# Conversions of low-rank weights and rotations of queries and keys, issued at later places and in program order

## The chip, the cores and the metric

One Trainium2 chip, one of its cores. The time is device microseconds (us) of one execution of the whole program, for an input of 256 tokens; lower is better. The engines: TensorE (PE in the profile; PEld is its weight load), VectorE (DVE), ScalarE (ACT), GpSimd (POOL) and SyncE (SP, whose queue issues all DMAs here).

## The reference

A trunk of two layers, 2048 wide. Each layer normalises, projects once, runs two groups of heads beside each other, gates both, projects back and adds:

```
for l in range(2):
    h = rms_norm(x, norm_g[l]);  proj = h @ w_in[l]
    rw_in, g_rw, q, k_at, v_at, g_at = split(proj)
    r, k, v, xw, xa = split(bidir_token_shift(rw_in, shift_mu[l]))
    # A) RWKV-7 mixing, one scan per direction d, 16 heads of 64
    decay = exp(-exp(-softplus(-(w0[d] + tanh(xw) @ decay_up[d])) - 0.5))   # decay_up: 96 x 1024
    a     = sigmoid(a0[d] + xa @ iclr_up[d])                                # iclr_up:  96 x 1024
    S = S*decay - (S@kk) (a*kk)^T + v k^T ;  y = S@r        # delta rule, forward and reversed, summed
    # B) windowed attention, 16 query heads, 4 key heads, sink logit
    qh, kh = rope(q), rope(k_at)        # [t1*cos - t2*sin, t2*cos + t1*sin] on halves of 32
    y_at = softmax_with_sink(qh kh^T / 8, |i-j| <= 128) @ v_at
    x = x + concat(y_rw * silu(g_rw), y_at * silu(g_at)) @ w_out[l]
out = rms_norm(x, final_g)
```

## The kernel before

Everything is kept transposed: 128 channels on the partitions, 256 tokens along the free axis. Every float32 product is made of three fp32r matmuls on a high and a low part of each operand: `hi` is a rounded copy made by ScalarE, `lo` = value − `hi`, made by VectorE.

**The stream of projections.** `gemm` is one output tile of 128 channels: 16 steps of three matmuls (L286 to L288) into one of two PSUM buffers `pm`. Its weights come in two halves of 512 KB (`raw<-wi`, three buffers), which `wsplit` turns into `hi` (L216, two calls of 128x512) and `lo` (L218), two buffers of each. `S.run(n)` issues the next n steps; `S.later(n, fn)` calls `fn` after the n-th step from there, the running one counted. When a tile's last step is issued its `evac` is called: it reads `pm` and frees it.

**The scans.** `window(64, ...)` issues 64 steps of the stream in 14 groups and between them the pieces of the scans: `scan_p` (decay, rates and keys of one pair of heads), `scan_i` (inverse of the triangular systems) and `scan_b` (state). Window w projects k, v, r and the gate of pair p = w; in it `scan_p` of pair w − 1 runs, so the low-rank product `pza` of pair w − 1 (L636 to L638) is some 16 steps into window w. `pza` is followed on ScalarE by `lw`, `th`, `t` and `kkr`, and on VectorE by a long chain from `lw<-lw` to the product behind `pbn`; PE needs `t` for `pk` (L642, first use) and the end of VectorE's chain for `pbn` (L642, second use). After the eight pairs come the tiles of k (two) and q (eight) of the attention, whose evacuation rotates them.

**What sets the order.** PE runs in program order. The other queues are ordered by a list scheduler, which places an instruction as soon as its model of the machine has the inputs ready and the engine free, the earlier in the program first. `PA` and `PV` are ScalarE and VectorE with one rule more: an instruction issued through them stays behind the instruction that the program issued before it on that engine. In the profile, all that goes through them has line L231. `scan_p` and part of the others use `PA` and `PV`.

**The two places of the change.** `ups` (L472) fetches the low-rank weights of a pair, `g<-iup` (96 rows) and `g<-dup` (97 rows), at the start of its k tile; `value_evac`, at the end of its v tile, evacuates v and converts both into `iuh`, `iu`, `duh`, `du` with `split` (L455 on ScalarE, L456 on VectorE). The buffers `g` are two, shared with the gates (`g`, `th` in `silu_evac`) and with the angles of `setup`, which make `SIN` and `COS` in window 0. `rope_evac` copies `pm` to `u` (L506), has four DMAs swap its halves into `rrot` (L508), turns on VectorE (L509 to L511) and converts (L513 on ScalarE, L514 on VectorE). All of these use the plain `A` and `V`.

Of the kernel before, what the change touches and what calls it, by code (L numbers as in the profile page):

```python
# [9 lines left out]
F32 = mybir.dt.float32  # L10
# [5 lines left out]
AF = mybir.ActivationFunctionType  # L16
ALU = mybir.AluOpType
# [112 lines left out]
def hybrid_trunk_kernel(ctx, tc, xT, wi, wv, wo, par, fing, dup, iup, sink, pos, cst, out):  # L130
    nc = tc.nc
    V, A, G, PE, SY = nc.vector, nc.scalar, nc.gpsimd, nc.tensor, nc.sync
# [22 lines left out]
    def st(tag, shape, dt=F32, bufs=1):  # L155
        return sp.tile([128, *shape], dt, tag=tag, name=tag, bufs=bufs)
# [76 lines left out]
    PA, PV = InTurn(A), InTurn(V)  # L233
# [36 lines left out]
    S = Stream()  # L270
# [130 lines left out]
    def queue_inputs(l):  # L401
# [7 lines left out]
        def shift_evac(j, place):  # L409
            def evac(pm):  # L410
                dst = place()
                u = st("u", [T], bufs=2)
                V.tensor_tensor(u, pm, L.norm.rb, op=ALU.mult)
                A.activation(dst, u, AF.Identity, scale=dpm(0, j))
                V.scalar_tensor_tensor(dst[:, 1:T], u[:, 0 : T - 1], prm(P_MU0, j), dst[:, 1:T], op0=ALU.mult, op1=ALU.add)
                V.scalar_tensor_tensor(dst[:, 0 : T - 1], u[:, 1:T], prm(P_MU1, j), dst[:, 0 : T - 1], op0=ALU.mult, op1=ALU.add)

            return evac
# [11 lines left out]
        def new(t, name, tag, bufs):  # L430
            def place():
                t[name] = st(tag, [T], bufs=bufs)
                return t[name]

            return place
# [17 lines left out]
        def split(hl, x, rows):  # L453
            hi, lo = (a[0:rows] for a in hl)
            A.activation(hi, x[0:rows], AF.Copy)  # L455
            V.tensor_tensor(lo, x[0:rows], hi.bitcast(F32), op=ALU.subtract)  # L456
# [19 lines left out]
        def value_evac(p, t):  # L476
            ev = shift_evac(8 + p, new(t, "v", "vg", 8))

            def evac(pm):
                ev(pm)  # L480
                for n, rows in (("iu", RANK), ("du", RANK + 1)):
                    raw = t[n]
                    t[n] = (st(n + "h", [2, 128], F32R), st(n, [2, 128], F32R))
                    split(t[n], raw, rows)

            return evac

# [9 lines left out]
        def rope_evac(place):  # L497
            def evac(pm):
                if not rope:
                    rope.extend((st("TW", [T]), st("XA", [T])))  # L500
                    V.tensor_tensor(rope[0], COS, L.norm.rb, op=ALU.mult)
                    V.tensor_tensor(rope[1], SIN, L.norm.rb, op=ALU.mult)
                CR, SR = rope
                raw = st("u", [T], bufs=2)
                rot = st("rrot", [T])
                A.activation(raw, pm, AF.Copy)  # L506
                for q in range(4):
                    SY.dma_start(out=rot[q * 32 : q * 32 + 32, :], in_=raw[(q ^ 1) * 32 : (q ^ 1) * 32 + 32, :])  # L508
                V.tensor_tensor(raw, raw, CR, op=ALU.mult)  # L509
                V.tensor_tensor(rot, rot, SR, op=ALU.mult)  # L510
                V.tensor_tensor(raw, raw, rot, op=ALU.add)  # L511
                hi, lo = place()
                A.activation(hi, raw, AF.Copy)  # L513
                V.tensor_tensor(lo, raw, hi.bitcast(F32), op=ALU.subtract)  # L514

            return evac

# [650 lines left out]
```

## Time and profile before

| | us |
|---|---|
| median of 3 runs | 1235.19 (1234.38 to 1235.47) |
| the profiled execution: its time | 1234.27 |
| its span | 1232.4 |
| PE busy | 1182.2 |
| DVE busy | 930.7 |
| ACT busy | 743.0 |
| DMA queue of SP, share of the 16 engines' span | 41.0% |

The span is the time from the first to the last instruction; 1.9 us lie around it. Rows of the timeline begin with start and duration in us; in brackets at the end is how long the engine had stood idle before and what ended that. In the rows by stretches, PEclk is the granted clock of TensorE as a share of full speed. A row of the waits gives the total in us, the number of times, and the longest.

### The profile page before, as it was taken

Reading aid. Unit: us, or ns where it says so; the run is one execution under the profiler, and the core shown is the slowest. Engines: PE = TensorE matmul, PEld = TensorE weight load, DVE = VectorE, ACT = ScalarE, POOL = GpSimd, SP = SyncE. Lnnn points to the kernel's source line nnn. Section 1 sums busy time; section 2 is a strip of 40 time slices with the busy share of each in tenths; the row PEclk is TensorE's granted clock in tenths of the full one; section 3 lists DMA queues with packets and bytes.
Section 4 is the critical chain, followed back from the end, with each engine's and each line's share of the span. In section 5 each row is a group of like instructions: output and inputs, shape, how many; then the busy total and the mean of one; then the engine's idle time right before and its main releaser. Section 6 shows DMA issues by size and latency. Waiting matters only on the chain. (4 is left out here: it accounts for less than half of the span.)

```text
span 1232.4 us, 38183 instructions
## 1 busy us (share of the span) xinstructions
PE 1182.2 (96%) x16204; PEld 1096.3 (89%) x16204; DVE 930.7 (76%) x2067; ACT 743.0 (60%) x1838; POOL 19.1 (2%) x23
## 2 busy tenths in 40 slices
PE   6989999999999899999998999999999999999996
PEld 6978998999998889999998889999999888899996
DVE  7878778887876668856676788878887866786654
ACT  6546665766665567655555556675776565665553
POOL 0000000000000000000000000000000000000000
PEclk9999999999999999999999999999999999999998
DMA  7433333323323334467654333333323333445653
GB/s 249 157 136 116 105 117 109 105 96 114 119 89 99 117 112 144 140 214 240 209 182 147 124 128 93 106 111 111 105 94 106 124 102 127 131 130 178 211 192 121
DMA packets 60411, 166.72 MB, mean 135 GB/s; under 512 B 7728, under 2 KB 22736, under 8 KB 60240
## 3 DMA queue, kind: packets, MB, share of 16 engines
q1 hardware_dynamic: 60240, 164.27, 41.0%
q8 instruction: 127, 2.08, 0.7%
q14 instruction: 44, 0.36, 0.1%
HBM read 157.43 MB, written 4.19 MB: 131 GB/s over the span
## 5 line engine op out<-in xcount | busy, mean ns | idle before, releaser
L286 PE MATMUL pm<-XH,hi 128*128 128x256 f32 x1664 | 498.8, 300 | 9.4 <-ACT XH L179 5.9
L288 PE MATMUL pm<-XH,lo 128*128 128x256 f32 x1664 | 471.5, 283 | 4.8 <-DVE lo L218 4.6
L287 PE MATMUL pm<-XL,hi 128*128 128x256 f32 x1664 | 471.8, 284 | 0.1
L216 ACT ACTIVATE hi<-raw 128x512 fp32r<-128x512 f32 x560 | 328.1, 625 | 238.0 <-PE pm L287 147.9
L218 DVE TENSOR_TENSOR lo<-raw,hi 128x512 fp32r<-128x512 f32 x560 | 368.4, 687 | 96.7 <-ACT hi L216 89.2
L286 PEld LDWEIGHTS pm<-XH,hi 128*128 128x128 f32 x1664 | 317.3, 191 | 34.9 <-issue 13.0
L288 PEld LDWEIGHTS pm<-XH,lo 128*128 128x128 f32 x1664 | 318.3, 191 | 6.5 <-DVE lo L218 6.4
L287 PEld LDWEIGHTS pm<-XL,hi 128*128 128x128 f32 x1664 | 318.3, 191 | 0.9 <-DVE XL L180 0.9
L286 PE MATMUL pm<-MH,hi 128*128 128x256 f32 x512 | 144.1, 281 | 1.2 <-ACT hi L216 1.2
L288 PE MATMUL pm<-MH,lo 128*128 128x256 f32 x512 | 143.9, 281 | 0.4 <-DVE lo L218 0.4
L287 PE MATMUL pm<-ML,hi 128*128 128x256 f32 x512 | 143.8, 281 | 0.0
L286 PEld LDWEIGHTS pm<-MH,hi 128*128 128x128 f32 x512 | 96.6, 189 | 2.2 <-ACT hi L216 1.4
L288 PEld LDWEIGHTS pm<-MH,lo 128*128 128x128 f32 x512 | 96.6, 189 | 0.6 <-DVE lo L218 0.6
L287 PEld LDWEIGHTS pm<-ML,hi 128*128 128x128 f32 x512 | 96.6, 189 | 0.0
L908 ACT ACTIVATE suv<-pcc 64x128 f32<-64x128 f32 x128 | 34.2, 267 | 18.1 <-PE pq L835 11.8
L837 ACT ACTIVATE QF<-pq 128x256 f16<-128x256 f32 x80 | 30.8, 385 | 19.8 <-PE pq L835 19.0
L993 ACT ACTIVATE mv<-mv,mx 128x257 f32<-128x257 f32 x64 | 32.0, 503 | 17.5 <-DVE mx L990 17.3
L740 DVE TENSOR_TENSOR ge<-pg,C 128x1024 f32<-128x1024 f32 x32 | 39.1, 1221 | 3.2 <-PE pg L734 3.1
L844 DVE CAST_PREDICATED tv<-LV,pd 128x256 f16<-128x256 uint8 x80 | 34.4, 430 | 7.7 <-PE pd L843 6.9
L892 ACT ACTIVATE rh<-pcc 128x128 f32<-128x128 f32 x64 | 17.5, 273 | 35.4 <-PE pcc L890 35.0
L734 PE MATMUL pg<-mv,bk 64*128 64x128 f32 x512 | 37.2, 285 | 0.0
L845 DVE CAST_PREDICATED tt<-LV,pd 128x256 f16<-128x256 uint8 x80 | 34.1, 426 | 0.0
(239 smaller groups left out, 1845.8 us busy)
## 6 DMA issues: line engine op xcount, KB each, us to landing
raw<-wi SPq DMA_DIRECT2D x207, 512.0 KB, 3.3
raw<-wo SPq DMA_DIRECT2D x64, 512.0 KB, 4.3
raw<-wv SPq DMA_DIRECT2D x8, 512.0 KB, 3.3
rrot<-u SPq DMA_DIRECT2D x80, 32.0 KB, 2.0
vg<-xT SPq DMA_DIRECT2D x16, 128.0 KB, 4.6
xd<-vg SPq DMA_DIRECT2D x16, 128.0 KB, 2.4
vg<-xd SPq DMA_DIRECT2D x16, 128.0 KB, 3.3
g<-dup SPq DMA_DIRECT2D x16, 97.0 KB
```

The lines of the kernel that those rows point to most:

```text
L216: A.activation(hi[:, q], raw[:, q], AF.Copy)
L218: V.tensor_tensor(lo[:, q], raw[:, q], hi[:, q].bitcast(F32), op=ALU.subtract)
L286: PE.matmul(pm, wh, rh[:, kk, :], start=(kk == 0), stop=False)
L287: PE.matmul(pm, wh, rl[:, kk, :], start=False, stop=False)
L288: PE.matmul(pm, wl, rh[:, kk, :], start=False, stop=(kk == 15))
L734: PE.matmul(pg[:, h, c * 128 : (c + 1) * 128], BK[half[h], d, c, 1 - h : 3 - h, :].rearrange("p s j -> p (s j)"), MV[half[h], d, c].rearra ...
L740: V.tensor_tensor(GEd(d), pg.rearrange("p h (c x) -> p h c x", c=NC), gm[d].unsqueeze(1).unsqueeze(1).to_broadcast([128, 2, NC, 128]), op= ...
L837: A.activation(t_sub(QF), flat4(pq[:, :, 0:128]), AF.Copy)
L844: V.copy_predicated(t_sub(TC), t_mask, flat4(pd[:, :, 0:128]))
L845: V.copy_predicated(v_sub(TT), v_mask, flat4(pd[:, 0, 128:384].rearrange("p (d x) -> p d x", d=2)))
L908: A.activation(here(h), pc[half[h], 1], AF.Copy)
L993: A.activation(Sc[:, h, q, 0:257], Sc[:, h, q, 0:257], AF.Exp, scale=0.125, bias=mx[:, q : q + 1], accum_out=den[:, q : q + 1])
```

## The change

The conversions of the low-rank weights are issued five steps after the evacuation of v instead of with it, and through `PA` and `PV`. The rotation is issued six steps after the copy to `u` and its conversion nine steps after, through `PA` and `PV` as well; the copy and the four DMAs stay. No instruction of a computation is added or removed.

```
         def value_evac(p, t):
             ev = shift_evac(8 + p, new(t, "v", "vg", 8))
-            def evac(pm):
-                ev(pm)
+            def parts():
                 for n, rows in (("iu", RANK), ("du", RANK + 1)):
                     raw = t[n]
                     t[n] = (st(n + "h", [2, 128], F32R), st(n, [2, 128], F32R))
-                    split(t[n], raw, rows)
+                    hi, lo = (a[0:rows] for a in t[n])
+                    PA.activation(hi, raw[0:rows], AF.Copy)
+                    PV.tensor_tensor(lo, raw[0:rows], hi.bitcast(F32), op=ALU.subtract)
+            def evac(pm):
+                ev(pm)
+                S.later(6, parts)
...
         def rope_evac(place):
                 A.activation(raw, pm, AF.Copy)
                 for q in range(4):
                     SY.dma_start(out=rot[q * 32 : q * 32 + 32, :], in_=raw[(q ^ 1) * 32 : (q ^ 1) * 32 + 32, :])
-                V.tensor_tensor(raw, raw, CR, op=ALU.mult)
-                V.tensor_tensor(rot, rot, SR, op=ALU.mult)
-                V.tensor_tensor(raw, raw, rot, op=ALU.add)
                 hi, lo = place()
-                A.activation(hi, raw, AF.Copy)
-                V.tensor_tensor(lo, raw, hi.bitcast(F32), op=ALU.subtract)
+                def turn():
+                    PV.tensor_tensor(raw, raw, CR, op=ALU.mult)
+                    PV.tensor_tensor(rot, rot, SR, op=ALU.mult)
+                    PV.tensor_tensor(raw, raw, rot, op=ALU.add)
+                def parts():
+                    PA.activation(hi, raw, AF.Copy)
+                    PV.tensor_tensor(lo, raw, hi.bitcast(F32), op=ALU.subtract)
+                S.later(7, turn)
+                S.later(10, parts)
```

PE's order stays. The order on ScalarE changes at the start of the first layer, where `rb` is the scale of the norm, which every evacuation there waits for. The rows of ScalarE before, with the conversions of pair 0:

```order
L1065 ACTIVATE mv<-X_87 128x1024
L216 ACTIVATE hi<-raw 128x512 x4
L455 ACTIVATE iuh<-g 96x256
L455 ACTIVATE duh<-g 97x256
L204 ACTIVATE rb<-pb 128x256
L216 ACTIVATE hi<-raw 128x512
```

And now:

```order
L1077 ACTIVATE mv<-X_87 128x1024
L216 ACTIVATE hi<-raw 128x512 x4
L204 ACTIVATE rb<-pb 128x256
L216 ACTIVATE hi<-raw 128x512
L414 ACTIVATE kr<-u,DP 128x256 x2
```

`rb` is no longer queued behind the two conversions; those now stand behind the evacuation of v of pair 0, `vg<-u`. In the second layer the pair that stood between the weight halves of the output projection went to the same place.

On ScalarE at the change from the first window to the second, in the first layer, the rows before were these (`duh` and `iuh` are pair 1's, `pza` is pair 0's):

```order
L358 ACTIVATE COS<-COS 128x256
L425 ACT_TABLE_LOAD
L425 ACTIVATE g<-g 128x256
L216 ACTIVATE hi<-raw 128x512 x4
L414 ACTIVATE kr<-u,DP 128x256
L455 ACTIVATE duh<-g 97x256
L455 ACTIVATE iuh<-g 96x256
L231 ACTIVATE lw<-pza 128x512
```

And now:

```order
L425 ACT_TABLE_LOAD
L425 ACTIVATE g<-g 128x256
L216 ACTIVATE hi<-raw 128x512 x2
L358 ACT_TABLE_LOAD
L358 ACTIVATE COS<-COS 128x256
L414 ACTIVATE kr<-u,DP 128x256
L231 ACT_TABLE_LOAD
L231 ACTIVATE lw<-pza 128x512
```

The two conversions have gone to a place behind `lw<-th`, fourteen rows further, and `COS` has come between the gate and `lw<-pza`, with two table loads more: the angles wait for the buffers `g`, which pair 0's conversions now free later. On VectorE `iu` and `du` of pair 1 have moved from ahead of `lw<-lw` into its chain, between `bk<-th` and `lw<-lw,kr`. The second layer has the same move without `COS` and the loads.

On VectorE at the first rotation of k (in each layer), before:

```order
L231 SCALAR_TENSOR_TENSOR lw<-lw,PR,kr 128x256
L509 TENSOR_TENSOR u<-u,TW 128x256
L510 TENSOR_TENSOR rrot<-rrot,XA 128x256
L932 TENSOR_SCALAR yv<-yv 128x4
L511 TENSOR_TENSOR u<-u,rrot 128x256
L231 TENSOR_TENSOR ysq<-py,yv 128x256
L218 TENSOR_TENSOR lo<-raw,hi 128x512
L514 TENSOR_TENSOR kd<-u,KA 128x256
L218 TENSOR_TENSOR lo<-raw,hi 128x512
L844 COPY_PREDICATED tv<-LV,pd 128x2x4x32
```

And now:

```order
L231 SCALAR_TENSOR_TENSOR lw<-lw,PR,kr 128x256
L231 TENSOR_TENSOR u<-u,TW 128x256
L231 TENSOR_TENSOR rrot<-rrot,XA 128x256
L944 TENSOR_SCALAR yv<-yv 128x4
L231 TENSOR_TENSOR u<-u,rrot 128x256
L218 TENSOR_TENSOR lo<-raw,hi 128x512 x2
L231 TENSOR_TENSOR kd<-u,KA 128x256
L231 TENSOR_TENSOR ysq<-py,yv 128x256
L856 COPY_PREDICATED tv<-LV,pd 128x2x4x32
```

The turn `u<-u,TW` stands where it stood; `ysq`, which waits for GpSimd's `yv`, has gone behind both weight halves and the conversion. On SP one weight load (`raw<-wi`) has moved ahead of the first fetch of pair 1 in the first layer, and in each layer one ahead of the four DMAs of the fourth rotation.

## The prediction

> **What bounds the kernel now.** I read the page's first part, then the waits of PE, then the timeline around the longest of them.
>
> ```profile
> span 1232.4 us, 38183 instructions
> PE 1182.2 (96%) x16204; PEld 1096.3 (89%) x16204; DVE 930.7 (76%) x2067; ACT 743.0 (60%) x1838; POOL 19.1 (2%) x23
> ```
>
> PE is busy for all but 50.2 us of the span, and its order and work don't change. So only its pauses, and a clock below full speed, can give time back.
>
> ```profile
> PE pbn L642 <- DVE lw L231: 5.6, 2, 2.8
> PE pk L642 <- ACT t L231: 5.4, 2, 2.9
> PE pm L288 <- DVE lo L218: 4.9, 7, 1.5
> PE pf L851 <- DVE tt L845: 3.5, 2, 2.4
> PE pq L835 <- DVE tv L844: 3.5, 4, 1.0
> PE pf L851 <- DVE tv L844: 2.7, 2, 1.5
> ```
>
> These are few and long, once or twice a layer. The timeline of PE says where they are:
>
> ```profile
> 29.28 0.38 PE L286 MATMUL pm<-XH,hi 128*128 128x256 f32 x1 [1.62 <-DVE u L413]
> 69.07 0.65 PE L642 MATMUL pk<-t,C 64*64 64x256 f32 x4 [2.92 <-ACT t L231]
> 85.59 0.65 PE L642 MATMUL pbn<-lw,C 64*64 64x256 f32 x4 [2.77 <-DVE lw L231]
> 548.36 0.39 PE L286 MATMUL pm<-MH,hi 128*128 128x256 f32 x1 [1.22 <-ACT hi L216]
> 549.24 0.38 PE L288 MATMUL pm<-MH,lo 128*128 128x256 f32 x1 [0.37 <-DVE lo L218]
> 669.07 0.65 PE L642 MATMUL pk<-t,C 64*64 64x256 f32 x4 [2.43 <-ACT t L231]
> 673.66 0.39 PE L288 MATMUL pm<-XH,lo 128*128 128x256 f32 x1 [1.45 <-DVE lo L218]
> 687.61 0.65 PE L642 MATMUL pbn<-lw,C 64*64 64x256 f32 x4 [2.78 <-DVE lw L231]
> ```
>
> What ScalarE and SP did just before:
>
> ```profile
> 28.08 0.42 ACT L455 ACTIVATE duh<-g 97x256 fp32r<-97x256 f32 x1 [4.59 <-DMA g<-dup]
> 66.70 0.42 ACT L455 ACTIVATE duh<-g 97x256 fp32r<-97x256 f32 x1 [4.38 <-DMA g<-dup]
> 547.38 0.42 ACT L455 ACTIVATE duh<-g 97x256 fp32r<-97x256 f32 x1 [4.50 <-DMA g<-dup]
> 666.69 0.42 ACT L455 ACTIVATE duh<-g 97x256 fp32r<-97x256 f32 x1 [3.94 <-DMA g<-dup]
> 59.07 0.30 SPq L472 DMA_DIRECT2D g<-dup  x1
> ```
>
> Each group of pauses follows one ScalarE conversion that stood waiting for its transfer: `g<-dup`, issued at 59.07, was waited for until 66.70, 7.6 us later. Behind it queued `rb` (first row), `lw<-pza` and `t` (second and fourth), the weight halves (third). These eight pauses are 15.6 us. The stretches show a second cost:
>
> ```profile
> 29.00:33.00 4.00, 3.72 (x18) 3.72 (x19) 3.88 (x11) 1.95 (x4) 0.00 (x0) 0.57 0.21 84
> 688.00:692.00 4.00, 4.00 (x25) 3.58 (x23) 0.72 (x2) 0.46 (x1) 0.00 (x0) 0.57 0.10 41
> ```
>
> The granted clock was 0.57 over these 4 us, so each costs PE 0.43 x 4 = 1.7 us. There are four, after the pauses at 29.28, 69.07, 673.66 and 687.61, of which the first and last are shown; not after 85.59.
>
> **The change part by part.** The sum is made against the profiled execution, 1234.27 us, which is 0.9 below the median of the runs.
>
> *First layer, start.* `rb` goes as soon as its product is there; what then stands ahead on VectorE is a cast, so I estimate the evacuation 1.2 of the 1.62 us earlier, and a pause of 0.4 left, too short for a lower clock among those seen: −1.2 − 1.7 = −2.9. Ends: 0 and −3.3.
>
> *First layer, pairs 0 and 1.* ScalarE's rows between the windows:
>
> ```profile
> 56.05 0.42 ACT L358 ACTIVATE COS<-COS 128x256 f32<-128x256 f32 x1 [0.81 <-DVE COS L357]
> 56.49 1.28 ACT L425 ACT_TABLE_LOAD   x1
> 57.78 0.42 ACT L425 ACTIVATE g<-g 128x256 f32<-128x256 f32 x1
> 60.76 1.15 ACT L216 ACTIVATE hi<-raw 128x512 fp32r<-128x512 f32 x2 [1.51 <-PE pm L287]
> 61.82 0.49 ACT L414 ACTIVATE kr<-u,DP 128x256 f32<-128x256 f32 x1
> 67.33 0.57 ACT L231 ACTIVATE lw<-pza 128x512 f32<-128x512 f32 x1
> ```
>
> VectorE's rows at its chain, and the busy times from the chain's start to just before `pbn`, in both layers:
>
> ```profile
> 68.22 0.42 DVE L231 TENSOR_SCALAR lw<-lw 128x512 f32<-128x512 f32 x1
> 667.88 0.41 DVE L456 TENSOR_TENSOR iu<-g,iuh 96x256 fp32r<-96x256 f32 x1
> 668.22 0.42 DVE L231 TENSOR_SCALAR lw<-lw 128x512 f32<-128x512 f32 x1
> 68.20:85.40 17.20, 13.74 (x100) 13.15 (x100) 16.85 (x31) 10.49 (x24) 0.00 (x0) 0.90 0.39 130
> 668.20:687.40 19.20, 14.28 (x100) 13.28 (x100) 16.70 (x31) 10.66 (x24) 0.00 (x0) 0.91 0.37 117
> ```
>
> PE is some 3.6 us earlier here (2.9, and part of the small waits for `lo`). The `hi` pair waits for PE, so it starts at 57.2 instead of 60.76. Then come a load, `COS`, `kr` and a load ahead of `lw<-pza`: 1.15 + 1.28 + 0.42 + 0.49 + 1.28, less 0.3 of overlap, = 4.3, so 61.5 instead of 67.33. The conversions were 5 us there; the two loads take 2.6 of it back. `lw<-lw` follows at 62.1 instead of 68.22, 6.1 earlier. From there VectorE was busy for 16.85 of 17.2 us to `pbn` at 85.59, 17.4 us after the start; the two conversions now inside add 0.34 each (667.88 to 668.22), 0.7 in all. So `pbn` comes 6.1 − 0.7 = 5.4 us earlier than 85.59, which contains the 2.9 of the start. It does not come when PE wants it: PE, 3.6 earlier still and without `pk`'s pause and slow stretch, is ready near 76, so the pause there grows to 3 or 4 us. That is longer than every pause after which the clock fell, so I add one slow stretch: −5.4 + 1.7 = −3.7. Ends: −11.6 (every pause and both stretches go) and 0.
>
> The Trainium skill, TensorE: Matmul & The Clock Gate, Part 1, puts the lower clock behind at least one idle window of about 3.4 us. The trace does not agree: the clock fell after 1.62 and 1.45 us. By that page the 1.7 at the start would not be gained, while a pause of 3 to 4 us keeps its stretch, and the sum would be 1223.4.
>
> *Output projection of the first layer.* The conversion leaves; nothing takes its place there, since ScalarE stood idle 4.50 us. −1.22 − 0.37 = −1.6; ends 0 and −2.
>
> *Second layer, pairs 0 and 1.* No loads here: `lw<-pza` follows `pza` at about 663.5, 3.9 before its place behind the conversions, and VectorE's chain starts 4.2 before 668.22. It is 0.7 longer, and part of the 2.5 us of idle time inside it (19.2 − 16.70) can now be filled by weight halves placed ahead of the reciprocal; I take −3.7, near its 3.5 and 4.2, at `pbn` (687.61). The slow stretch after 673.66 lies inside that span, the one after 687.61 stays with its longer pause. Ends: −10.1 (2.43 + 1.45 + 2.78 + 2 x 1.7) and 0.
>
> *Pairs 2 to 7.* The conversions move from ahead of `lw<-pza` to later in the same window, twelve times. No pause of PE there hangs on them; their cover is the `lo` buffers, a half tile ahead. 0; ends ±2.
>
> *Rotations.* Twenty, all with the same four DMAs.
>
> ```profile
> 374.01 0.43 DVE L509 TENSOR_TENSOR u<-u,TW 128x256 f32<-128x256 f32 x1 [2.19 <-DMA rrot<-u]
> 376.14 0.42 DVE L231 TENSOR_TENSOR ysq<-py,yv 128x256 f32<-128x256 f32 x1 [0.90 <-POOL yv L933]
> 378.82 0.30 PE L851 MATMUL pf<-tv,NEYE 64*64 64x256 f16 x4 [2.43 <-DVE tt L845]
> 401.54 0.45 PE L890 MATMUL pcc<-suv,ge 128*64 128x64 f32 x8 [1.28 <-DVE suv L915]
> ```
>
> The first turn still stands at the same place in VectorE's queue, so its 2.19 us wait for the DMA stays. What goes is the 0.90 wait behind it: the two weight halves run while GpSimd works. So `tt` comes about 1.0 earlier, in each layer −1.0; at the third q tile, the same, −0.5 each. At 401.54 `suv` loses two instructions of 0.34 ahead of it: −0.6 each. At the fourth rotation a weight load now issues ahead of the four DMAs, which have to wait for its buffer: +0.3 each. Sum −3.6; the later ones, from the fifth on, 0, since there only short waits are seen. Ends: −8.5 (all waits for `tt`, `tv` and `suv` above and half of those for `pq`) and +3. What a conversion waits for next is its partner on the other engine, 0.4 us away by the rows of that size.
>
> Sum: −3.7 − 1.6 − 3.7 + 0 − 3.6 = −12.6, so 1234.3 − 12.6 = 1221.7; beside the median, up to 0.9 more. I say 1222.
>
> **Rivals.**
> 1. *All pauses go.* VectorE's 24% of idle time takes the chain in, and `pbn` waits for nothing: −11.6 − 2.0 − 10.1 − 8.5 = −32, 1202 us. Against it: in the first layer VectorE has 0.35 us of gaps between 68.2 and 85.4. 0.07.
> 2. *The late transfer only moves.* `g<-dup` takes 7.6 us; if its issue slips behind the extra weight load, `du` inside the chain waits again, and both `pbn` pauses eat what `pk` gave. Left are 2.9 at the start less the added stretch 1.7, the 1.6 and the rotations' 3.6: 1228 us. Against it: by the estimates above some 9 us lie between its issue and the new place. 0.10.
> 3. *Rotations give nothing.* Their DMA waits stay and only change owner: 1225.3 us. 0.15.
> 4. *Table loads are dearer than their row.* If each of the two new switches also held the engine for as long as the load, `lw<-pza` is 2.6 later: 1224.3 us. Against it: the load at 56.49 starts 0.02 after the activation before it, and the next one (57.78) 0.01 after the load. 0.08. The Trainium skill, ScalarE: Activation LUTs, What ACT_TABLE_LOAD costs, gives 2.66 us for a switch, half of it draining.
> 5. *Slower.* Turns and conversions, held in order, make VectorE stand before weight halves that PE needs. At 0.9 us (the wait of `ysq`, 376.14) for each of twenty rotations that is 18 us against the 9.0 of the other terms: 1243 us. It decides from 0.45 us each on. Against it: VectorE stood 2.2 us at 374.01 already, and PE felt it in a few places only. 0.05.
>
> **How the numbers follow.** The forecast has 0.55; with it the rivals make 1. From 1213 (not quite half of what rival 1 adds) to 1230 lie the forecast, 2, 3 and 4; outside are 1, 5 and some of the tails of 2, 0.17 together. Less than 0.2% (2.5 us) cannot be told from no change in this kernel. Slower takes rival 5, 0.05; same 0.05, from 2 going on to no gain; faster the rest, 0.90.
>
> **What would show it.** No `duh` row waiting for `g<-dup`; no pause at `pk`; a pause at `pbn` of 3 us or more in both layers, with a granted clock near 0.57 behind it; five table loads instead of three; `ysq` behind two `lo` at the first rotation, with the DMA wait at `u` still there. It is wrong if `pbn` does not wait, if new waits for `lo` appear in the attention's windows, or if `g<-dup` is waited for at its new place.

## The result and the profile after

The changed kernel took 1223.09 us (median of 4 runs, 1220.40 to 1224.15) against 1235.12 us of the kernel before; the ratio is 0.9904, 95% interval 0.9887 to 0.9920. The forecast was 1222, range 1213 to 1230. The profiled execution is the fastest of the four: 1220.40 us with a span of 1218.6.

The page's first part and the waits of PE, after (waited for: us in total, times, longest us):

```profile
span 1218.6 us, 38161 instructions
PE 1177.0 (97%) x16204; PEld 1092.3 (90%) x16204; DVE 929.5 (76%) x2067; ACT 747.6 (61%) x1840; POOL 19.1 (2%) x23
```

```profile
PE pbn L654 <- DVE lw L231: 8.2, 2, 4.1
...
PE pq L847 <- DVE tv L856: 5.8, 4, 1.6
...
PE pk L654 <- ACT t L231: 1.6, 1, 1.6
```

PE's busy time fell by 5.2 us with the same 16204 matmuls. Two slow stretches fewer (pieces of 3.41 us at half the granted clock) are 3.4 of it; the rest was not followed. Waits for `pbn` grew from 5.6 to 8.2, those for `pk` fell from 5.4 to 1.6. The timeline of PE at the places of the prediction (each bracket is the pause just before the row):

```profile
27.77 0.38 PE L286 MATMUL pm<-XH,hi 128*128 128x256 f32 x1 [0.31 <-DVE u L413]
63.15 0.65 PE L654 MATMUL pk<-t,C 64*64 64x256 f32 x4 [1.60 <-ACT t L231]
79.94 0.65 PE L654 MATMUL pbn<-lw,C 64*64 64x256 f32 x4 [4.11 <-DVE lw L231]
115.51 0.30 PE L847 MATMUL pq<-tv,AB 64*64 64x32 f16 x16 [1.63 <-DVE tv L856]
373.36 0.30 PE L863 MATMUL pf<-tv,NEYE 64*64 64x256 f16 x4 [0.36 <-DVE tt L857]
674.63 1.12 PE L654 MATMUL pbn<-lw,C 64*64 64x256 f32 x4 [4.11 <-DVE lw L231]
```

ScalarE around the first window's end, after. `duh` has no wait behind it any more; two more table loads stand ahead of `lw<-pza`:

```profile
40.99 0.40 ACT L231 ACTIVATE duh<-g 97x256 fp32r<-97x256 f32 x1
...
57.95 1.28 ACT L358 ACT_TABLE_LOAD   x1
59.24 0.42 ACT L358 ACTIVATE COS<-COS 128x256 f32<-128x256 f32 x1
59.57 0.49 ACT L414 ACTIVATE kr<-u,DP 128x256 f32<-128x256 f32 x1
60.08 1.28 ACT L231 ACT_TABLE_LOAD   x1
61.37 0.60 ACT L231 ACTIVATE lw<-pza 128x512 f32<-128x512 f32 x1
```

VectorE's chain in the first layer, after: its start, the two conversions inside it, and the busy times of the stretch (PE, PEld, DVE, ACT, POOL, then PE's granted clock):

```profile
62.00 0.43 DVE L231 TENSOR_SCALAR lw<-lw 128x512 f32<-128x512 f32 x1 [0.90 <-ACT lw L231]
72.12 0.41 DVE L231 TENSOR_TENSOR iu<-g,iuh 96x256 fp32r<-96x256 f32 x1
73.06 0.42 DVE L231 TENSOR_TENSOR du<-g,duh 97x256 fp32r<-97x256 f32 x1
```

```profile
62.00:79.80 17.80, 12.68 (x100) 11.80 (x100) 17.34 (x32) 11.54 (x26) 0.00 (x0) 1.00 0.47 157
80.70:84.70 4.00, 4.00 (x27) 3.78 (x29) 0.92 (x3) 0.81 (x2) 0.00 (x0) 0.58 0.10 42
```

VectorE is busy for 17.34 of 17.80 us while PE waits at its end, and the lower clock (0.58) follows.

PE issues the same matmuls in the same order in both kernels, so the start of the same matmul can be compared. The table gives how far it moved from one place to the next, against the terms of the sum. The value to 119.23 includes 0.19 us that the first transfers were faster in this execution:

| stretch, by times of the kernel before | forecast | measured |
|---|---|---|
| start, pairs 0 and 1 of the first layer (to 119.23) | −3.7 | −3.73 |
| of this, to 40.08 (the wait for `rb` and the clock behind it) | −2.9 | −3.05 |
| pairs 2 to 7 (to 365.08) | 0 | +0.34 |
| rotations, first layer (to 459.45) | −1.8 | −3.48 |
| output projection (to 549.46) | −1.6 | −2.27 |
| pairs 0 and 1 of the second layer (to 723.00) | −3.7 | −3.42 |
| to 970.01 | 0 | +0.34 |
| rotations, second layer (to 1060.57) | −1.8 | −1.44 |
| to the last matmul | 0 | −0.13 |
| sum | −12.6 | −13.79 |

The sum is nearer than its parts: the rotations of the first layer gave 1.7 us more than forecast and the output projection 0.7 more, while two stretches with a term of 0 lost 0.34 each and two of the second layer fell short by 0.3 and 0.4.

### The profile page after: what moved, and what is told of

Read it like the earlier page. It is cut to its first block, busy times and chain, and to the rows that moved or that the text cites. A ratio compares the mean times of both kernels' runs of the same rounds, so it can differ in the third digit from the quotient of the medians.

```text
span 1218.6 us, 38161 instructions
## 1 busy us (share of the span) xinstructions
PE 1177.0 (97%) x16204; PEld 1092.3 (90%) x16204; DVE 929.5 (76%) x2067; ACT 747.6 (61%) x1840; POOL 19.1 (2%) x23
## 5 line engine op out<-in xcount | busy, mean ns | idle before, releaser
L752 DVE TENSOR_TENSOR ge<-pg,C 128x1024 f32<-128x1024 f32 x32 | 39.1, 1222 | 5.0 <-PE pg L746 5.0
```

The lines of the kernel that those rows point to most:

```text
L752: V.tensor_tensor(GEd(d), pg.rearrange("p h (c x) -> p h c x", c=NC), gm[d].unsqueeze(1).unsqueeze(1).to_broadcast([128, 2, NC, 128]), op= ...
```

## Experiments

All were timed against the kernel before on their own chip. Its median lay between 1233.5 and 1235.0 there, single runs between 1229.75 and 1239.02, so kernels of different chips are compared by the ratios.

| kernel | us, median | ratio to before, 95% interval |
|---|---|---|
| after_again | 1223.99 | 0.9906 (0.9888 to 0.9923) |
| convs_only | 1227.99 | 0.9951 (0.9931 to 0.9970) |
| rope_only | 1229.59 | 0.9962 (0.9946 to 0.9979) |
| no_pin | 1232.78 | 0.9990 (0.9977 to 1.0002) |
| pin_at_once | 1229.09 | 0.9955 (0.9939 to 0.9971) |
| table_free | 1225.22 | 0.9920 (0.9904 to 0.9936) |
| behind_chain | 1218.33 | 0.9864 (0.9845 to 0.9883) |
| turn_later | 1224.35 | 0.9912 (0.9895 to 0.9929) |
| bonus_later | 1211.56 | 0.9818 (0.9798 to 0.9837) |
| two_queues | 1224.81 | 0.9924 (0.9907 to 0.9942) |
| angles_later | 1226.38 | 0.9943 (0.9927 to 0.9958) |
| bonus_9 | 1228.18 | 0.9959 (0.9944 to 0.9974) |

### One half alone: convs_only and rope_only

Each is the kernel before with one of the two hunks of the diff: `value_evac` alone, or `rope_evac` alone.

> Only the conversions of the low-rank weights are moved; queries and keys are turned as before. Theory (the parts are independent, since PE's pauses of the one lie in pairs 0 and 1 and the output projection, those of the other in the rotations): the trace of after was 12.3 us ahead of before outside the rotations' stretches, less the 3.5 and 1.4 it gained inside them: 8.9 us, so about 1226 us against 1235.1, with a pause of 4 us at pbn in both layers, 1.6 at pk in the first, none at the output projection, and the rotations' pauses of before (2.4 for tt, 1.3 for suv, 1.5 and 1.2 for tv). Rival 1 (the rotations carried the gain): 1232 or more. Rival 2 (the conversions carry all of it): 1223.

> Only the rotations of queries and keys are moved; the conversions of the low-rank weights stay as before. Theory: 4.9 us less than before (3.5 in the first layer, 1.4 in the second, as the two traces differ between the last matmul ahead of the rotations and the first lo behind them), so about 1230 us; the forecast on record had 3.6, 1231.5. The pauses at rb (1.6), pk (2.9 and 2.4), pbn (2.8 twice) and the output projection (1.2) are all there again. Rival (the rotations give nothing by themselves, what they gained came from elsewhere): 1235.

The halves add up: 0.0049 and 0.0038 make 0.0087, the whole change measured 0.0096 and 0.0094. rope_only came where it was expected. convs_only gave 5.9 us (1233.9 to 1228.0) and not 8.9. Its pauses are those expected (1.59 at `pk`, 4.11 and 4.12 at `pbn`); the price of the clock behind them is not. The first stretch is of after, the second of convs_only (the column before the last two is the granted clock):

```profile
78.00:90.00 12.00, 10.06 (x94) 8.98 (x94) 6.56 (x12) 2.30 (x5) 0.00 (x0) 0.86 0.37 131
```

```profile
78.00:90.00 12.00, 9.39 (x69) 8.06 (x70) 6.67 (x13) 1.50 (x4) 0.00 (x0) 0.72 0.40 135
```

The same pause of 4.11 us was followed by 0.14 x 12 = 1.7 us lost in one and 0.28 x 12 = 3.4 in the other. The expectation had read 8.9 us from one profiled execution, in which three slow stretches lay before the end; the kernel before had five in its own. With half of every slow stretch taken off, the last matmul moved by 5.1 us in convs_only and 5.6 in rope_only (start transfers set equal at the matmul at 14.05), 10.2 in after: additive within 0.5 us.

### What does it: the hold in program order, or the later place?

```diff
 no_pin:       PA.activation / PV.tensor_tensor -> A. / V. in both parts()
               and in turn(), the S.later calls stay
 pin_at_once:  S.later(6, parts) -> parts();  S.later(7, turn) -> turn();
               S.later(10, parts) -> parts(), PA and PV stay
```

> Both parts are issued later in the program (6, 7 and 10 steps), but without being held in program order on ScalarE and VectorE. Theory: the scheduler moves the conversions forward to where they stood before (iuh and duh ahead of rb again), so ScalarE waits 4 to 5 us for g<-dup as before and the pauses at rb, pk, pbn and the output projection return; the gain of some 9 us from the conversions is gone and what is left is that of the rotations, 0 to 5 us: 1230 to 1235. Rival (the later place alone does it, the hold in order is not needed): 1223, like after.

> Both parts are held in program order on their engines, but issued at once, where the code of before issues them (no later). Theory: for the conversions the hold alone is enough, since behind the evacuation of the value tile the transfer has landed (duh without a wait, pairs 0 and 1 within 0.5 us of after); the turn, held right behind its four transfers, makes VectorE wait some 2 us for them in each of twenty rotations, with everything behind it, so the 4.9 us gained in the rotations are gone or become a loss: 1226 to 1232. Rival 1 (the hold does everything): 1223. Rival 2 (held at once, the conversions wait for the transfer again): 1232 or more, with duh rows that wait for g<-dup.

Without the hold, the scheduler moved the conversions forward to where they had stood, and ScalarE waited again, four times (no_pin):

```profile
28.37 0.42 ACT L484 ACTIVATE duh<-g 97x256 fp32r<-97x256 f32 x1 [4.10 <-DMA g<-dup]
65.25 0.42 ACT L484 ACTIVATE duh<-g 97x256 fp32r<-97x256 f32 x1 [4.06 <-DMA g<-dup]
546.45 0.42 ACT L484 ACTIVATE duh<-g 97x256 fp32r<-97x256 f32 x1 [3.60 <-DMA g<-dup]
664.79 0.42 ACT L484 ACTIVATE duh<-g 97x256 fp32r<-97x256 f32 x1 [3.78 <-DMA g<-dup]
```

Its ratio cannot be told from 1. Held but issued at once, no `duh` row waits, and pairs 0 and 1 moved by 3.55 us to 119.23, as in after (3.54, both from 14.05 on). So for the conversions the hold does it all, and the 6 steps nothing. At the first rotation it is the other way. In no_pin, later but not held, `ysq` (377.56) stands behind two `lo` and the conversion and waits for nothing. In pin_at_once GpSimd's result is waited for again, 0.90 us, and PE's pause there is 1.46 instead of 0.36:

```profile
373.07 0.42 DVE L231 TENSOR_TENSOR ysq<-py,yv 128x256 f32<-128x256 f32 x1 [0.90 <-POOL yv L945]
375.75 0.30 PE L863 MATMUL pf<-tv,NEYE 64*64 64x256 f16 x4 [1.46 <-DVE tt L857]
```

### after_again and table_free

```diff
-        ang = st("g", [T], bufs=2)
-        nn = st("g", [T], bufs=2)
+        ang = st("t1", [T], bufs=3)
+        nn = st("t1", [T], bufs=3)
```

> The changed kernel once more, beside the variants on the same chip. Theory (the two parts are additive, and the granted clock's share scatters around the same mean in all kernels): the ratios of the two halves, 0.9951 and 0.9962, add up to 0.991, so 0.9900 to 0.9925 to the kernel before, some 11 us. Rival (the first measurement's 0.9904 was helped by the clock, of which its profiled execution lost only three windows): 0.993 or more.

> The changed kernel with the angles of the position tables in buffers of another name, so that they don't wait for the buffers of the low-rank weights: three table loads instead of five, the two of 1.28 us ahead of lw<-pza are gone. Theory (VectorE's chain from lw<-lw to pbn is what PE waits for, and it starts when ScalarE has made lw): lw<-pza 2.6 us earlier, no pause at pk (1.6 in after), pbn some 2.6 us earlier with a pause of about 3.1 instead of 4.1: 2.6 us less than after, a ratio near 0.9885. Rival 1 (VectorE is full there anyway, so the chain ends when it did): the 1.6 at pk moves to pbn, pause 5.7, no change against after. Rival 2 (each load holds ScalarE for twice its row): 5 us less.

The repeat gave 0.9906, near the 0.9913 of the two halves together. Its profiled execution was 4.20 us longer than the first one of the same kernel, 1224.60 against 1220.40; its start transfers took 0.91 more (the matmul at 14.05) and it had five slow stretches instead of three (3.4 us): 4.3.

table_free lost the pause at `pk` and the two loads and gained nothing. The theory failed: the angles' rows, back at their earlier place in VectorE's queue, made PE wait for `lo` ahead of `pk` (the matmul at 60.04 of before started at 58.01, in after_again at 56.73). VectorE's chain started earlier, at 61.58 against 63.09, but then stood 1.43 us for `pk` itself, and it ended for PE as late as ever (`pbn` at 81.02 in after_again):

```profile
48.87 0.38 PE L288 MATMUL pm<-XH,lo 128*128 128x256 f32 x1 [0.46 <-DVE lo L218]
81.29 1.12 PE L654 MATMUL pbn<-lw,C 64*64 64x256 f32 x4 [4.10 <-DVE lw L231]
```

### behind_chain

```diff
-                S.later(6, parts)
+                S.later(6 if p == 0 else 20, parts)
```

> The changed kernel with the conversions of pairs 1 to 7 issued 20 steps instead of 6 behind their value tile, so behind VectorE's chain and not inside it. Theory (the two conversions cost the chain 0.67 us in each of the places where PE waits for it): pbn's pause 4.1 to 3.4 in both layers, pq's pause at 115.5 and 710.2 from 1.63 to the 0.96 of before: 2.7 us less than after, a ratio near 0.988. Rival 1 (what leaves the chain is filled by weight halves placed ahead): pbn as in after, at most 1.3 us. Rival 2 (the new place delays others): new pauses behind bv or at the next pair's pza, no gain.

5.7 us less than after_again, twice what was expected. The timeline of PE:

```profile
79.87 1.12 PE L654 MATMUL pbn<-lw,C 64*64 64x256 f32 x4 [3.81 <-DVE lw L231]
117.78 0.65 PE L654 MATMUL pbn<-lw,C 64*64 64x256 f32 x4 [0.29 <-DVE lw L231]
674.34 1.12 PE L654 MATMUL pbn<-lw,C 64*64 64x256 f32 x4 [4.12 <-DVE lw L231]
```

`pbn` of pair 0 kept most of its pause, but not because weight halves filled the place of the conversions (rival 1): ten `lo` rows lie in the first layer's chain as in after. From `lw<-lw` to `pbn` it took 17.36 us (62.51 to 79.87) instead of 17.93 in after_again, and 19.01 instead of 19.67 in the second layer, close to the 0.67 of the theory. In the second layer the gain shows as a wait of PE for `lo` ahead of `pbn` that fell from 0.72 to 0.06, so PE came to `pbn` earlier as well. `pq` (at 115.5 and 710.2 in after) lost the whole of its 1.63, not 0.67, for 0.29 at the `pbn` of pair 1; why it was the whole was not followed. The profile has four slow stretches before the end and after_again's five: 1.7 of the 5.8 us between these two executions.

### turn_later and two_queues

```diff
 turn_later:  S.later(7, turn) -> S.later(10, turn);  S.later(10, parts) -> S.later(13, parts)
 two_queues:  SY.dma_start(out=rot[...  ->  (SY if q < 2 else A).dma_start(out=rot[...
```

> The changed kernel with the turn 10 and its conversion 13 steps behind, instead of 7 and 10. Theory (VectorE's waits for the four transfers of a rotation, 20.7 us in twelve places in after, still reach PE through tt and tv): three steps are 2.6 us, more than eleven of the twelve waits, so these nearly go; of PE's pauses behind them (0.36, 0.94, 0.79, 1.57, 0.45: 4.1) most go: 3 us less than after, a ratio near 0.988. Rival 1 (PE's pauses there have other causes, VectorE would have idled anyway): within 1 us of after. Rival 2 (turn and conversion collide with other work at the later place): up to 3 us slower than after.

> The changed kernel with two of the four transfers of each rotation issued from ScalarE's queue, the other two from SP's. Theory (the turn waits for the four issues in a row on SP, 3.2 us for the four at 364.95 in after and 3.8 in before, more than for the transfer itself): the last half lands some 1.6 us earlier, VectorE's waits for rrot<-u fall from 20.7 us to 8 or less, PE's pauses behind them (4.1) by half: 2 to 3 us less than after, a ratio of 0.988. Rival 1 (the issues hold ScalarE for as long as they held SP, and delay the weight halves): waits for hi and lo instead, 0 to 3 us slower than after. Rival 2 (the transfer, not the issue, is what is waited for): waits and time as in after.

Neither gained. In turn_later the waits for `rrot<-u` came to 23.9 us, not near 0: the scheduler left the first turn where it was, and the conversions that had covered GpSimd's time went behind `ysq`:

```profile
372.06 0.43 DVE L231 TENSOR_TENSOR u<-u,TW 128x256 f32<-128x256 f32 x1 [2.37 <-DMA rrot<-u]
374.18 0.42 DVE L231 TENSOR_TENSOR ysq<-py,yv 128x256 f32<-128x256 f32 x1 [0.90 <-PE pm L287]
376.52 0.30 PE L863 MATMUL pf<-tv,NEYE 64*64 64x256 f16 x4 [2.25 <-DVE tt L857]
```

(The 0.90 is GpSimd's, as in the other kernels; the row names another engine.) At this one place twelve of the fourteen traces show a pause of PE, and they follow one line: it is the wait for the transfer, plus 0.9 where `ysq` waits, less 0.7 (1.0 in turn_later). Before: 2.19 + 0.90 gave 2.43; convs_only 1.47 + 0.90 gave 1.71; after 1.11 gave 0.36; no_pin 2.03 gave 1.28; table_free 2.46 gave 1.73. The transfer's part scatters between 0.88 and 2.46 from trace to trace (0.72 in two_queues); at 0.88 (behind_chain) and 0.72 no pause is listed.

two_queues shortened SP's issues there from 3.22 us for four to 1.25 for two, and the waits at most turns, but their sum only fell from 20.7 to 19.7 us. Three turns of q waited longer than in after, 4.14, 3.96 and 2.26 us. At the first of them the two issues held ScalarE's queue for 2.05 us, and PE then waited for ScalarE's `suv`:

```profile
416.69 2.05 ACTq L513 DMA_DIRECT2D rrot<-u  x2
```

```profile
422.07 0.43 DVE L231 TENSOR_TENSOR u<-u,TW 128x256 f32<-128x256 f32 x1 [4.14 <-DMA rrot<-u]
```

```profile
425.36 0.45 PE L925 MATMUL pcc<-suv,bt 128*64 128x64 f32 x8 [1.39 <-ACT suv L920]
```

That the issues caused that wait is read from the order of the rows, not tested.

### bonus_later

On top of behind_chain, pair 0's last product is issued six projection steps later:

```diff
+            def bonus():
+                pb = wbank("pbn")
+                head_sums(pb, km)
+                bv = t["bv"] = st("bv", [T], bufs=3)
+                PV.tensor_tensor(bv, pb[:, 0:T], VV, op=ALU.mult)
+            if p == 0:
+                S.later(6, bonus)
+            else:
+                bonus()
```

> behind_chain (1218.3 us, ratio 0.9864) with one more edit: for pair 0 of each layer the two products pbn and what follows them are issued 6 steps of the projections later, so PE does six steps (some 5 us) of other work where it stood 3.8 and 4.1 us. This changes PE's order. Theory (the pause at pbn is PE's order: the next projections could go on while VectorE ends its chain): no pause over 1 us there, no lower clock behind it; 3.8 + 4.1 less some new short waits for lo of 1 us in all, and two to four windows of the lower clock at 1.7 each: 9 to 13 us less than behind_chain, 1206 to 1210, ratio near 0.978. Rival 1 (VectorE is short of time there, the projections would wait for their lo instead): the same 4 us as waits at pm for lo, at most 2 us gained. Rival 2 (pair 0's later stages, pg above all, are delayed by it): new pauses there, 0 to 5 us gained.

1211.56 us. Against behind_chain, which ran on another chip, the ratio fell by 0.0046, 5.7 us (6.8 between the medians): the theory in kind, and short of its 9 to 13. PE, in the first layer and the second, and the stretch after the first (granted clock 1.00):

```profile
80.63 0.65 PE L654 MATMUL pbn<-lw,C 64*64 64x256 f32 x4 [0.89 <-DVE lw L231]
83.65 1.16 PE L753 MATMUL pg<-mv,bk 64*128 64x128 f32 x16 [1.10 <-DVE ge L759]
670.69 0.65 PE L654 MATMUL pbn<-lw,C 64*64 64x256 f32 x4 [0.79 <-DVE lw L231]
673.70 1.16 PE L753 MATMUL pg<-mv,bk 64*128 64x128 f32 x16 [1.10 <-DVE ge L759]
```

```profile
76.00:88.00 12.00, 10.01 (x112) 8.60 (x112) 9.41 (x18) 5.72 (x15) 0.00 (x0) 1.00 0.47 158
```

The pauses of 3.81 and 4.12 became two of about 1 each (the expectation allowed 1 us in all; those at `pg` are what its rival 2 named), and the clock stayed up: one slow stretch before the end, at 15.59, against four in behind_chain, 5.1 us of the 7.5 between the two profiled executions. This is the best version: 0.9818 against 0.9906 for the change as it was.

### angles_later and bonus_9

On top of bonus_later, the sines and cosines are computed in the window of pair 4; bonus_9 adds three steps to `bonus`.

```diff
-        posi = st("t1", [T], I32, bufs=3)
+        posi = COS.bitcast(I32)
-            [(setup_, [2, 5])] if l == 0 and w == 0
+            [(setup_, [5])] if w == 0, [(setup_, [2])] if w == 4   (first layer; masks first, angles last)
-                S.later(6, bonus)
+                S.later(9, bonus)                                  (bonus_9 only)
```

> bonus_later (1211.6 us, ratio 0.9818) with the sines and cosines of the positions computed three windows of pairs later (in the window of pair 4 instead of pair 0; the positions wait in the buffer of the cosines). Theory (in table_free the shift of 2.6 us at lw<-pza was paid back because the angles' rows came early into VectorE's full stretch around 40 to 55 us; here they leave both stretches, and the table loads too): no pause at pk (1.6), no more waits at lo ahead of it, pbn of pair 0 not later than PE wants it: 1.6 to 3 us less than bonus_later in the first layer alone, 1208.5 to 1210, ratio 0.979 to 0.9805. Rival 1 (VectorE's chain is the end in any case): the 1.6 turns up at pbn, whose pause of 0.9 becomes 2.5, and the time stays at 1211.6. Rival 2 (the loads and the angles hurt where they now stand): a new pause in the window of pair 4, at most 2 us, and 1211 to 1213.

> angles_later with pair 0's pbn 9 steps later instead of 6. Theory (what pauses are left at pbn and pg, 0.8 to 1.1 each, four in all, come from VectorE's order around bv and ge, and pbn at 9 steps stands at its old place against pg): the pauses of 0.8 to 0.9 at pbn go, those at pg stay: 0.8 to 1.7 us less than angles_later. Rival (nothing left to gain, the waits move to pg): within 0.5 us of angles_later.

Locally the theory held: between the matmuls at 29.28 and 119.23 PE gained 9.0 us against 7.7 in bonus_later, with no pause at `pk`. But rival 2's price was far too small. In the window of pair 4 (angles_later), ScalarE, VectorE and PE:

```profile
208.40 1.28 ACT L425 ACT_TABLE_LOAD   x1 [2.34 <-DVE COS L359]
209.70 0.42 ACT L425 ACTIVATE g<-g 128x256 f32<-128x256 f32 x1
210.13 1.28 ACT L369 ACT_TABLE_LOAD   x1
211.43 0.42 ACT L369 ACTIVATE COS<-COS 128x256 f32<-128x256 f32 x1
211.75 0.40 ACT L231 ACTIVATE MH<-t 128x256 fp32r<-128x256 f32 x1
```

```profile
212.18 0.42 DVE L231 TENSOR_TENSOR ML<-t,MH 128x256 fp32r<-128x256 f32 x1 [1.61 <-ACT MH L231]
```

```profile
213.25 0.26 PE L875 MATMUL pf<-tv,AL 64*64 64x64 f16 x1 [12.51 <-DVE AL L231]
```

`MH` is held in program order and stands behind the cosine, which waits for two dozen rows of VectorE; `ML` waits for `MH`, and `AL`, held behind `ML`, for both; PE stood 12.51 us, and the lower clock was granted from 201.84 to 218.90. From 160 to 250 (times of before) the matmuls fell back by 16.6 us. bonus_9 shows the same, and in the first layer its pause at `pbn` only moved to `pg` (2.16).

## Why the prediction was right, point by point

- *First layer, start.* Forecast −2.9, measured −3.05: the pause is 0.31 (0.4 was said) and the slow stretch behind it is gone.
- *First layer, pairs 0 and 1.* `lw<-pza` was forecast at 61.5 and `lw<-lw` at 62.1; they stand at 61.37 and 62.00. `pbn` came 5.65 earlier (5.4 was said), with a pause of 4.11 (3 to 4) and the clock at 0.58 behind it. The chain to `pbn` grew from 17.37 to 17.94, 0.57 (0.7 was said). One sign failed: "no pause at `pk`". PE came there 4.6 us earlier, not 3.6, and stood 1.60. Part of this is that the waits for `lo` of 0.22 and 0.70 at 52.66 and 55.06 in before are gone; they came back in another place in table_free, where the angles stand early again. The pause of 4.11 then came near its forecast by luck: 82.82, where PE was ready in before, less 3.6, less `pk`'s 2.92 and the stretch's 1.7 is 74.6, not "near 76", and leaves a pause of 5.6 before 80.2. Measured were 1.60 and 4.11, 5.71 together. The sum goes by when `pbn` starts and does not hang on this. With VectorE busy for 17.34 of 17.80 us, a shorter pause at `pk` would only have made the one at `pbn` longer; this is argued, since in table_free, where `pk` has none, PE lost the time to `lo`.
- *Rival 4, table loads.* The load at 60.08 starts 0.02 after the row ahead of it has ended (59.57 + 0.49), and the rows behind the two loads start 0.01 after them (59.24 and 61.37). The Trainium skill, ScalarE: Activation LUTs, What ACT_TABLE_LOAD costs, adds a drain about as long as the load; no row here shows one. `lw<-pza` at 61.37 and not 64.1 excludes this rival.
- *Output projection.* The pauses of 1.22 and 0.37 went, as said; 0.7 more went in that stretch, which was not followed.
- *Second layer, pairs 0 and 1.* −3.42 against −3.7, pause 4.11 against about 4.6.
- *Pairs 2 to 7.* The term was 0, but in each layer the two conversions of pair 2 stand ahead of `tv`, and PE's pause at `pq` grew by 0.67 (0.96 became 1.63). The matmul at 119.23 is this `pq`, so in the table the loss lies in the stretches to 119.23 and 723.00. behind_chain took more than all of it back; the 0.34 of the stretches behind was not followed. The cover that the prediction named was that of the weight halves; it did not look at `tv`.
- *Rotations.* −3.6 was the term, −4.92 in the traces, 4.7 in rope_only. The mechanism at the first one is as said: `ysq` stands behind a `lo` pair and the rotation's own conversion and waits no more, which is worth 0.9; pin_at_once, convs_only and turn_later, where it stands ahead of them, pay it. What was wrong in size is the wait for the transfer in the first layer: 2.19 us were said to stay, it was 1.11 in this execution, and it scatters. So 1.1 of the −3.48 is luck of this execution. The other places have the signs forecast: the pauses at `suv` went from 1.28 and 0.49 to 0.13 and 0.13, those for `tv` at the third q tile from 1.47 and 1.25 to 0.79 and 0.45, while `pq` rose from 0.57 and 0.97 to 0.94 and 1.57.

VectorE's rows at the first rotation, after:

```profile
369.54 0.42 DVE L231 TENSOR_TENSOR u<-u,TW 128x256 f32<-128x256 f32 x1 [1.11 <-DMA rrot<-u]
370.68 1.29 DVE L218 TENSOR_TENSOR lo<-raw,hi 128x512 fp32r<-128x512 f32 x2
371.89 0.42 DVE L231 TENSOR_TENSOR kd<-u,KA 128x256 fp32r<-128x256 f32 x1
372.22 0.42 DVE L231 TENSOR_TENSOR ysq<-py,yv 128x256 f32<-128x256 f32 x1
```

- *Rival 2* did not occur: `g<-dup` is waited for nowhere. *Rival 3* is excluded by rope_only. *Rival 5* did not occur in this change, but its mechanism, work held in order behind a late row, is what cost angles_later 16.6 us.
- *The clock.* Five slow stretches before the end in the profile of before, three after: the net two that the sum takes off. This part of the agreement owes something to the execution: after_again had five. One stretch was charged behind each `pbn`; behind the same pause of 4.1 us it was one piece in after and two in convs_only, in both layers.

## What to carry to other kernels

In this kernel the conversions had to be held where their transfer has landed; calling them later in the program was not enough, since the scheduler moved them forward. Holding is not free either, since the held work stands behind whatever late row precedes it (angles_later). When PE waits for the end of another engine's full chain, look first at whether PE has other work to do in that time: six steps of projections ahead of `pbn` gave 0.0046 of the time, as much as the best change to the places of the conversions (0.0042, behind_chain against after_again). A gain of a few us read from one profile should be split into pauses and clock before it is trusted.

## What the runs showed of the hardware

The lower clock came in pieces of 3.413 us on a fixed grid: in the profile of before the pieces start at 15.90, 29.55, 70.51, 674.67 and 688.32, whole multiples of 3.413 apart. In the fourteen traces PE's idle time was added up for each interval of this grid from the first on record (some 12 us after the start) to the end phase. After 45 of 45 intervals with more than 1.75 us of it the next was slow, after 16 of 41 between 1.35 and 1.75, and after 4 of 4827 with less; these four were slow themselves. So about half an interval is enough, and whether a pause of 1.6 to 4.1 us costs nothing, 1.7 or 3.4 depends on where it lies: 2.77 us at 85.59 in before were split 1.34 and 1.43 and cost nothing, 1.62 at 29.28 lay inside one and cost 1.7. The first slow piece starts at 15.90 in before, 15.77 in after and 16.79 in after_again, so the grid lies elsewhere in each execution. That agrees with the Trainium skill, TensorE: Matmul & The Clock Gate, Part 1, which calls the window free-running. Its condition for the lower clock, at least one idle window, does not fit these traces, where about half of one was enough.

Four transfers of one rotation held SP's queue for 3.2 to 3.8 us in all at 364.95 (after) and 368.35 (before), longer than the 1.9 to 2.0 us (median) in which such a transfer lands. At most of the twenty rotations it was 2.41 or 2.42.
